# Other order of the loads, sums and transposes in the prologue of a hybrid conv and mLSTM block

## The chip, the cores and the metric

The kernel runs on one core of a Trainium2 chip. The metric is the device time of one execution in microseconds (us), lower is better; the time of a kernel is the median of its runs. In the rows, PE is TensorE's matrix multiplication, PEld its loading of weights, DVE VectorE, ACT ScalarE, POOL GpSimd, SP the engine that issues the DMAs. All times in rows count from the start of the profiled span.

## What is computed

One decoder block over x of 1024 tokens by 1024 channels, in float32. Only its beginning matters here:

```
mod = silu(c) @ w_ada + b_ada
sh1, sc1, g1, sh2, sc2, g2 = split(mod, 6)
h = rms_norm(x, norm_mix_g) * (1.0 + sc1) + sh1
proj = h @ w_in + b_in
```

`proj` feeds a gated convolution of 31 taps, an mLSTM over chunks and two gates; their merged output goes through `w_out`, and a SwiGLU feed-forward and a last RMSNorm follow. All that comes after the first columns of `proj` is the same text in both kernels.

## The kernel before

The channels lie on the 128 partitions, in 8 tiles of 128, and the 1024 tokens run along a row. Every large product is made three times: the left and the right operand are split into a high part of type float32r and the rest, named `hh` and `hl` for h, `whi` and `wlo` for weights (`wf` for the first two weight tiles), and high by high, high by low and low by high are added up.

The prologue makes `hh` and `hl` of h, and with them the first two column tiles of `proj`, so that the steady part, which begins with the products of L165, finds everything ready. It has these steps.

- **x**: four DMAs of 1 MB bring x, 256 tokens each, into the pairs `xt` (`xt_104` and `xt_106` hold the first 512 tokens, the other two the second). ScalarE squares each of the 8 token tiles with a sum along the row (L242, an ACTIVATE and an ACTIVATION_READ_ACCUMULATOR each). For each half of four tiles VectorE prepares the means (`rstd`, L244), GpSimd takes the power -0.5 (L111), and the four tiles are scaled in place (L251 on VectorE; the last of the eight on ScalarE, L249).
- **Transposes**: TensorE turns each half into channel tiles, four 128 by 128 transposes for each of the 8 channel tiles k (L255), into three PSUM buffers: one `pn` for k = 0, 3 and 6, two `pc` for the others. They are copied from there into the half rows of `xT` (L258), on ScalarE or VectorE as the letters of `EVAC` say, one string for each half.
- **Modulation**: `w_ada` for shift and scale is loaded in four groups g of 256 channels for each of the two (`wad`, 2 MB a group in four DMAs: rows 0 to 511 and 512 to 1023, for shift and for scale). VectorE sums a group's 8 row tiles, each times silu(c), into `macc` (the first at L282, the other seven at L284, each on top of the one before). TensorE sums the partitions with a column of ones (L290, the column products, 8 rows in the trace for 4 products), and ScalarE makes columns of shift and scale of that (L299, L300).
- **h**: for the two channel tiles of each group ScalarE makes `hh` (L304) and the full h in place (L307), VectorE subtracts the two into `hl` (L343). For the last group VectorE makes the full h (L347). The first two weight tiles are split into `wf`, high part on ScalarE (L155), low part on VectorE (L156).
- **First products**: for each group, 16 matmuls of `hh` (L315), then the next group's column products, then 8 matmuls of `hl`.

A scheduler orders each engine's instructions by readiness and priority; in the prologue the lists `on_v`, `on_s` and `on_t` are tied one behind the other (`in_turn`) for VectorE, ScalarE and TensorE. On the chip each engine takes its instructions in the order of the program. SP issues the loads in this order: the first two pairs of x, c, the last two pairs, `b_ada` and `mix_g`, the four DMAs of group 0 of `w_ada`, two weight tiles (`wraw`), then the groups 1 to 3.

Of the kernel before, what the change touches and what calls it, by code (L numbers as in the profile page):

```python
# [8 lines left out]
F32 = mybir.dt.float32  # L9
# [3 lines left out]
OP = mybir.AluOpType  # L13
# [3 lines left out]
D = 1024  # L17
# [18 lines left out]
EVAC = ("aaaaaaaa", "avaavaav")  # L36
# [19 lines left out]
def hybrid_block(ctx: ExitStack, tc: tile.TileContext, x, c, w_ada, b_ada, norm_mix_g, w_in, b_in,  # L56
# [140 lines left out]
    for i in range(4):  # L197
        t = pro.tile([128, 2, D], F32, name=f"xt{i}", tag=f"xt{i}")
        nc.sync.dma_start(t, x2[i * 256:(i + 1) * 256, :].rearrange("(a p) d -> p a d", p=128))
        xt += [t[:, 0, :], t[:, 1, :]]  # L200
    wad = []

    def load_ada(g):
        t = pro.tile([128, KT, 2, 256], F32, name="wad", tag="wad", bufs=4)
        for kh in range(2):
            for i in range(2):
                c0 = i * 1024 + g * 256
                nc.sync.dma_start(t[:, kh * 4:kh * 4 + 4, i, :],
                                  wada[kh * 512:(kh + 1) * 512, c0:c0 + 256].rearrange("(k p) e -> p k e", p=128))
        wad.append(t)  # L210
# [10 lines left out]

    def split_rest():
        for i in range(2):
            load_split(None, 0, KT, 0, *w_first[i], raw=raws[i])
# [11 lines left out]
    late_evac = {"v": [], "s": []}  # L236
    rstd = pro.tile([128, 3, 8], F32, name="rstd")
    xT = [big.tile([128, S], F32, name=f"xT{k}", tag="xb") if k < XB else pro.tile([128, S], F32, name=f"xT{k}") for k in range(KT)]
    for q in range(2):
        for t in range(4 * q, 4 * q + 4):  # L240
# [5 lines left out]
        for t in range(4 * q, 4 * q + 4):  # L246
            r = rstd[:, 1, t:t + 1]
            if SCALE[t] == "a":
                nc.scalar.activation(xt[t], xt[t], AF.Copy, scale=r)  # L249
            else:  # L250
                (nc.gpsimd if SCALE[t] == "p" else nc.vector).tensor_scalar(xt[t], xt[t], r, None, op0=OP.mult)  # L251
        for k in range(KT):
            p = ps_n() if k % 3 == 0 else ps_c()
            for t in range(4):
                nc.tensor.transpose(p[:, t * 128:(t + 1) * 128], xt[q * 4 + t][:, k * 128:(k + 1) * 128], ident)  # L255
            h = xT[k][:, q * 512:(q + 1) * 512]
            e = "s" if EVAC[q][k] == "a" else "v"
            ins = nc.scalar.activation(h, p, AF.Copy) if e == "s" else nc.vector.tensor_copy(h, p)  # L258
            if q and k > 1:
                late_evac[e].append(ins)  # L260
# [15 lines left out]

    def mod_sums(g):
        acc = pro.tile([128, 2, 256], F32, name="macc", tag="macc", bufs=MACC)
        parts = [[], []]
        for k in range(KT):  # L280
            if k < 1:
                ins = nc.vector.tensor_scalar(acc, wad[g][:, k], sc_c[:, k:k + 1], None, op0=OP.mult)  # L282
            else:
                ins = nc.vector.scalar_tensor_tensor(acc, wad[g][:, k], sc_c[:, k:k + 1], acc, op0=OP.mult, op1=OP.add)  # L284
            parts[k // 4].append(ins)
        return acc, parts
# [32 lines left out]
    on_v, on_s, on_t = [], [], []  # L319
    w_next = [None]  # L320
    hl = []
    acc, parts = mod_sums(0)
    on_v.append(parts[1])
    on_v.append(late_evac["v"])
    on_s.append(late_evac["s"])
    split_rest()
# [1191 lines left out]
```

## Time and profile before

| | |
|---|---|
| median of 3 runs | 1707.31 us (1704.89 to 1707.32) |
| the profiled execution | 1706.31 us, its span 1704.6 us |
| TensorE busy in the span | 1664.8 us (98%) |
| VectorE busy | 1310.5 us (77%) |
| ScalarE busy | 647.5 us (38%) |
| GpSimd busy | 59.5 us (3%) |
| start of the steady products (L165) | 61.55 us |

Shares over the whole span say little of the prologue, which is its first 61.55 us: there each engine has to be read by itself, in order of time, with what ended its idle time.

### The profile page before, as it was taken

How to read it: one execution, taken by the hardware profiler on the slowest of the kernel's cores; microseconds unless marked ns; L12 is line 12 of the kernel's file. 1: busy time of each engine (PE TensorE's matmuls, PEld its weight loads, DVE VectorE, ACT ScalarE, POOL GpSimd, SP SyncE). 2: the span in 40 equal slices, each digit the busy share in tenths (PEclk: the TensorE clock that was granted, in tenths of full speed). 3: DMA queues.
4: the chain of work that ended last, by engine and by line, in shares of the span. 5: the costliest groups of instructions: out<-in, count | busy, mean ns of one | idle time of the engine just before them, and what ended most of it. 6: DMA issues, size and time to landing. Idle time of an engine off the chain costs nothing. (4 is left out here: it accounts for less than half of the span.)

```text
span 1704.6 us, 20805 instructions
## 1 busy us (share of the span) xinstructions
PE 1664.8 (98%) x8237; PEld 1394.9 (82%) x8237; DVE 1310.5 (77%) x1760; ACT 647.5 (38%) x835; POOL 59.5 (3%) x116
## 2 busy tenths in 40 slices
PE   5999999999999999999999999999999999999998
PEld 4798888888888889888888778888888888788886
DVE  6989998997699759637699567877767777667776
ACT  7425335322532253224521356422222222344344
POOL 0000001000000000000000000000000000000001
PEclk9999999999999999999999999999999999999999
DMA  9221121122112211224497543333332333495872
GB/s 325 64 63 49 38 62 38 50 62 75 38 39 73 62 38 50 75 82 155 129 374 283 189 160 130 112 105 100 99 104 93 101 98 110 144 355 188 283 248 110
DMA packets 221241, 211.12 MB, mean 124 GB/s; under 512 B 8455, under 2 KB 175127, under 8 KB 221143
## 3 DMA queue, kind: packets, MB, share of 16 engines
q1 hardware_dynamic: 202327, 164.70, 31.3%
q10 hardware_dynamic: 18576, 44.31, 6.9%
q8 instruction: 64, 1.05, 0.3%
q0 software_dynamic: 240, 0.79, 0.1%
q14 instruction: 34, 0.28, 0.0%
HBM read 168.60 MB, written 41.16 MB: 123 GB/s over the span
## 5 line engine op out<-in xcount | busy, mean ns | idle before, releaser
L395 DVE SCALAR_TENSOR_TENSOR cacc<-a,col,cacc 128x1024 f32<-128x1024 f32 x240 | 306.1, 1282 | 3.9 <-ACT cacc L393 1.4
L165 PE MATMUL mm<-hh,wlo 128*128 128x512 f32 x864 | 271.2, 391 | 1.6 <-DVE wlo L156 1.6
L165 PE MATMUL mm<-hl,whi 128*128 128x512 f32 x864 | 272.5, 392 | 0.0
L165 PE MATMUL mm<-hh,whi 128*128 128x512 f32 x864 | 271.6, 392 | 0.0
L165 PEld LDWEIGHTS mm<-hh,wlo 128*128 128x128 f32 x864 | 160.4, 188 | 33.7 <-DVE wlo L156 2.8
L165 PEld LDWEIGHTS mm<-hl,whi 128*128 128x128 f32 x864 | 161.0, 188 | 32.1 <-issue 0.5
L165 PEld LDWEIGHTS mm<-hh,whi 128*128 128x128 f32 x864 | 160.5, 188 | 31.6
L155 ACT ACTIVATE whi<-wraw 128x1024 fp32r<-128x1024 f32 x61 | 64.7, 1060 | 227.4 <-PE mm L165 176.1
L156 DVE TENSOR_TENSOR wlo<-wraw,whi 128x1024 fp32r<-128x1024 f32 x61 | 74.3, 1219 | 28.7 <-ACT whi L155 25.2
L1123 PE MATMUL mm<-Bh,gh 128*128 128x512 f32 (+1 forms) x192 | 71.5, 375 | 2.8 <-ACT gh L1060 1.4
L1124 PE MATMUL mm<-Bl,gh 128*128 128x512 f32 (+1 forms) x192 | 71.5, 373 | 0.7 <-DVE Bl L1042 0.7
L611 PE MATMUL mm<-wlo,hh 128*128 128x256 f32 x256 | 72.0, 282 | 0.0
L1125 PE MATMUL mm<-Bh,gl 128*128 128x512 f32 (+1 forms) x192 | 71.2, 371 | 0.0
L1215 ACT ACTIVATE wd<-reg 128x1024 fp32r<-128x1024 f32 (+1 forms) x36 | 35.2, 988 | 82.6 <-DVE reg L1339 54.2
L542 DVE SCALAR_TENSOR_TENSOR cacc<-qkraw,col,cacc 128x1024 f32<-128x1024 f32 x48 | 61.5, 1281 | 4.9 <-ACT cacc L540 4.5
L1366 PE MATMUL mm<-wd,xl 128*128 128x512 f32 (+1 forms) x154 | 59.6, 387 | 1.2 <-DVE xl L1347 1.2
L1365 PE MATMUL mm<-wd,xh 128*128 128x512 f32 (+1 forms) x154 | 59.6, 387 | 0.0
L1367 PE MATMUL mm<-wd,xh 128*128 128x512 f32 (+1 forms) x154 | 59.5, 386 | 0.0
L610 PE MATMUL mm<-whi,hh 128*128 128x256 f32 x192 | 54.5, 284 | 0.0
L612 PE MATMUL mm<-whi,hl 128*128 128x256 f32 x192 | 54.2, 283 | 0.0
L1347 DVE TENSOR_TENSOR xl<-xr,xh 128x1408 fp32r<-128x1408 f32 x27 | 43.7, 1619 | 8.7 <-ACT xh L1346 8.7
L1216 DVE TENSOR_TENSOR wd<-reg,wd 128x1024 fp32r<-128x1024 f32 (+1 forms) x36 | 40.2, 1132 | 11.2 <-ACT wd L1215 11.0
(501 smaller groups left out, 3863.8 us busy)
## 6 DMA issues: line engine op xcount, KB each, us to landing
wraw<-in_w_in_dram SPq DMA_DIRECT2D x64, 512.0 KB
xr<-act_d SPq DMA_DIRECT2D x27, 704.0 KB
awt<-in_w_ada_dram SPq DMA_DIRECT2D x32, 512.0 KB
graw<-in_w_ffn_up_dram SPq DMA_DIRECT2D x24, 512.0 KB
act_d<-cg ACTq DMA_DIRECT2D x48, 256.0 KB
uraw<-in_w_ffn_up_dram SPq DMA_DIRECT2D x22, 512.0 KB
reg<-in_w_ffn_down_dram SPq DMA_DIRECT2D x20, 512.0 KB
other<-in_w_ffn_down_dram SPq DMA_DIRECT2D x20, 512.0 KB
```

The source lines that it names most:

```text
L155: nc.scalar.activation(hi, raw, AF.Copy)
L156: (eng or nc.vector).tensor_sub(lo, raw, hi.bitcast(F32))
L165: nc.tensor.matmul(flat(acc)[:, a:b], lhs[:, k, :], rhs[k][:, a:b], start=(first and k == 0), stop=(last and k == kt - 1))
L395: nc.vector.scalar_tensor_tensor(acc, a[:, j:j + S], dw_col(j, ct), acc, op0=OP.mult, op1=OP.add)
L542: nc.vector.scalar_tensor_tensor(cv, raw[:, j:j + S], wcol(j), cv, op0=OP.mult, op1=OP.add)
L611: nc.tensor.matmul(o[:, 0:256], hh[k][:, ts_], los[k], start=False, stop=False)
L1123: nc.tensor.matmul(o, a, rh, start=(k == 0), stop=False)
L1124: nc.tensor.matmul(o, a, rl, start=False, stop=False)
L1125: nc.tensor.matmul(o, b, rh, start=False, stop=(k == 3))
L1365: nc.tensor.matmul(o, xh, wh, start=(k == 0), stop=False)
L1366: nc.tensor.matmul(o, xl, wh, start=False, stop=False)
L1367: nc.tensor.matmul(o, xh, wl, start=False, stop=(k == FP - 1))
```

## The change

Five things are moved. The first half of `w_ada`'s group 0 is loaded between the first and the second half of x, the second half of it behind x in quarters. Group 0 is summed in two parts: four row tiles directly behind the first half's scaling, the others between the scalings of the second half. The squares of the second half are tied behind the first half's last evacuation on ScalarE, and their roots are taken for two tiles at a time. The evacuations are dealt out in another way: of the first half four of eight go to VectorE (none before), of the second half one (three before). The high parts of `wf` are made by VectorE. And of the second half's transposes, k = 0 to 2 stand ahead of the column products of group 0, k = 3 to 5 behind them, and k = 6 and 7 behind the first 16 products.

```diff
-EVAC = ("aaaaaaaa", "avaavaav")
+EVAC = ("avavavav", "avaaaaaa")
...
+    def ada_rows(t, g, k0, n):
+        for i in range(2):
+            c0 = i * 1024 + g * 256
+            nc.sync.dma_start(t[:, k0:k0 + n, i, :],
+                              wada[k0 * 128:(k0 + n) * 128, c0:c0 + 256].rearrange("(k p) e -> p k e", p=128))
...
+    x_pair(0)
+    x_pair(1)
     param_columns(param_rows(6, [("b_ada", as_rows(b_ada, 48), 48), ("mix_g", as_rows(norm_mix_g, 8), 8)], rows[:, 1]))
-    load_ada(0)
+    ada0 = ada_tile()
+    ada_rows(ada0, 0, 0, 4)
+    x_pair(2)
+    x_pair(3)
+    ada_rows(ada0, 0, 4, 2)
+    ada_rows(ada0, 0, 6, 2)
...
+    def roots(a, b):
+        for t in range(a, b):
             junk = ps_mm()
-            nc.scalar.activation(flat(junk), xt[t], AF.Square, accum_out=rstd[:, 0, t:t + 1])
-        ms, rs, sc = (rstd[:, i, 4 * q:4 * q + 4] for i in range(3))
-        nc.vector.tensor_scalar(ms, ms, 1.0 / D, EPS, op0=OP.mult, op1=OP.add)
+            ins = nc.scalar.activation(flat(junk), xt[t], AF.Square, accum_out=rstd[:, 0, t:t + 1])
+            if t == 4:
+                queue_behind(ins, turned_s[-1])
+        ms, rs = (rstd[:, i, a:b] for i in range(2))
+        ins = nc.vector.tensor_scalar(ms, ms, 1.0 / D, EPS, op0=OP.mult, op1=OP.add)
+        if a == 4:
+            queue_behind(ins, turned_v[-1])
         rsqrt(rs, ms)
...
+    roots(0, 4)
+    for t in range(4):
+        scale(t)
+    for k in range(KT):
+        turn(0, k)
+    acc = mod_sums(0, range(4))
+    roots(4, 6)
+    scale(4)
+    scale(5)
+    mod_sums(0, range(4, 6), acc)
+    roots(6, 8)
+    scale(6)
+    scale(7)
+    mod_sums(0, range(6, 8), acc)
...
-    split_rest()
+    for k in range(3):
+        turn(1, k)
     p, ins = mod_products(0, acc)
+    on_t.append(ins)
+    for i in range(2):
+        on_v.append([nc.vector.tensor_copy(w_first[i][0], raws[i])])
+    for i in range(2):
+        on_v.append([nc.vector.tensor_sub(w_first[i][1], raws[i], w_first[i][0].bitcast(F32))])
...
             on_s.append([high(k)])
+            if g == 0:
+                for j in ((3,), (4, 5))[k]:
+                    turn(1, j)
...
         on_t.append(first_products(g, 0))
+        if g == 0:
+            turn(1, 6)
+            turn(1, 7)
```

`turn(q, k)` is one channel tile of one half: its four transposes and its evacuation. `scale`, `mod_sums` and the other functions do what the lines before did; VectorE's parts of them are put into `on_v` in the order of the text.

On VectorE, between the scaling of the first half of x and the sums of group 1 of the modulation, this stood before (from the roots of the second half on; `xT` is x transposed):

```order
L244 TENSOR_SCALAR rstd<-rstd 128x4
L282 TENSOR_SCALAR macc<-wad,sc_c 128x512
L251 TENSOR_SCALAR xt_108<-xt_108,rstd 128x1024 x2
L251 TENSOR_SCALAR xt_110<-xt_110,rstd 128x1024
L284 SCALAR_TENSOR_TENSOR macc<-wad,sc_c,macc 128x512 x4
L258 COPY xT_149<-pc 128x512
L284 SCALAR_TENSOR_TENSOR macc<-wad,sc_c,macc 128x512
L156 TENSOR_TENSOR wf_125<-wraw,wf_124 128x1024
L284 SCALAR_TENSOR_TENSOR macc<-wad,sc_c,macc 128x512
L156 TENSOR_TENSOR wf_129<-wraw,wf_128 128x1024
```

Two more sums' parts and two evacuations follow there until group 1. In the changed kernel the same stretch of VectorE ends with these rows, ahead of the sums of group 1:

```order
L277 COPY xT_157<-pc 128x512
L260 TENSOR_SCALAR rstd<-rstd 128x2
L270 TENSOR_SCALAR xt_118<-xt_118,rstd 128x1024 x2
L292 SCALAR_TENSOR_TENSOR macc<-wad,sc_c,macc 128x512
L260 TENSOR_SCALAR rstd<-rstd 128x2
L292 SCALAR_TENSOR_TENSOR macc<-wad,sc_c,macc 128x512
L270 TENSOR_SCALAR xt_120<-xt_120,rstd 128x1024
L292 SCALAR_TENSOR_TENSOR macc<-wad,sc_c,macc 128x512 x2
L277 COPY xT_151<-pc 128x512
L365 CAST wf_126<-wraw 128x1024
L365 CAST wf_130<-wraw 128x1024
L367 TENSOR_TENSOR wf_127<-wraw,wf_126 128x1024
```

The roots and the scaling of the second half now stand behind the last evacuation of the first half (the copy into `xT_157`, which is k = 7), the sums' second part is dealt out around them, and two casts of a weight tile are new ahead of the subtractions.

On ScalarE, behind the first half's squares, the second half's squares came first before, and then the evacuations:

```order
L242 ACTIVATE mm,rstd<-xt_108 128x1024 x2
L242 ACTIVATE mm,rstd<-xt_110 128x1024 x2
L258 ACTIVATE xT_148<-pn 128x512
L258 ACTIVATE xT_149<-pc 128x512
L258 ACTIVATE xT_150<-pc 128x512
L249 ACTIVATE xt_110<-xt_110,rstd 128x1024
```

In the changed kernel the same place on ScalarE reads:

```order
L277 ACTIVATE xT_150<-pn 128x512
L277 ACTIVATE xT_152<-pc 128x512
L277 ACTIVATE xT_154<-pc 128x512
L277 ACTIVATE xT_156<-pn 128x512
L256 ACTIVATE mm,rstd<-xt_118 128x1024 x2
L256 ACTIVATE mm,rstd<-xt_120 128x1024 x2
L268 ACTIVATE xt_120<-xt_120,rstd 128x1024
```

The squares moved behind the four evacuations that ScalarE keeps of the first half (k = 0, 2, 4, 6), the last of which needs TensorE's transposes of k = 6. From the first products of the last group on, the order of all five engines is the same in both kernels.

## Rows read from the trace of the kernel before

**Rows 1.** Busy time of each engine (and instructions) in the prologue and in all that follows; the last columns are the granted clock of TensorE as a share of 2.4 GHz, the share of the DMA engines' time and GB/s.

```profile
0.00:61.55 61.55, 43.37 (x199) 34.14 (x199) 47.02 (x74) 44.66 (x69) 2.96 (x10) 0.94 0.78 247
61.55:1704.60 1643.05, 1621.39 (x8040) 1360.75 (x8039) 1263.47 (x1686) 602.85 (x766) 56.56 (x106) 1.00 0.37 119
```

**Rows 2.** VectorE in order of time from the last evacuation ahead of group 1 on: start, time from the first one's start to the last one's end, what, number, and in brackets the idle time ahead and what ended it (no bracket: none worth a row). The sums of the groups 1 and 2 begin at 28.77 and 37.13.

```profile
27.57 1.28 DVE L258 COPY xT<-pc 128x512 f32<-128x512 f32 x2
28.77 0.47 DVE L282 TENSOR_SCALAR macc<-wad,sc_c 128x512 f32<-128x512 f32 x1
29.27 5.48 DVE L284 SCALAR_TENSOR_TENSOR macc<-wad,sc_c,macc 128x512 f32<-128x512 f32 x7
34.67 2.55 DVE L343 TENSOR_TENSOR hl<-xT,hh 128x1024 fp32r<-128x1024 f32 x2
37.13 0.48 DVE L282 TENSOR_SCALAR macc<-wad,sc_c 128x512 f32<-128x512 f32 x1
...
43.04 2.55 DVE L343 TENSOR_TENSOR hl<-xT,hh 128x1024 fp32r<-128x1024 f32 x2
```

**Rows 3.** Busy time of VectorE (and instructions) in the stretch from the sums of group 1 to the end of the last subtraction of the prologue; then clock, DMA share and GB/s as in Rows 1.

```profile
28.77:60.27 31.50, 30.44 (x39) 0.89 0.57 173
```

**Rows 4.** VectorE in order of time ahead of that, from the first half's roots on.

```profile
10.71 0.17 DVE L244 TENSOR_SCALAR rstd<-rstd 128x4 f32<-128x4 f32 x1 [1.31 <-ACT mm L242]
12.03 2.74 DVE L251 TENSOR_SCALAR xt<-xt,rstd 128x1024 f32<-128x1024 f32 x4 [1.15 <-POOL rstd L111]
15.31 0.22 DVE L135 COPY col<-pa 128x56 f32<-128x56 f32 x1 [0.55 <-PE pa L132]
...
16.39 0.17 DVE L244 TENSOR_SCALAR rstd<-rstd 128x4 f32<-128x4 f32 x1 [0.38 <-ACT mm L242]
16.77 0.49 DVE L282 TENSOR_SCALAR macc<-wad,sc_c 128x512 f32<-128x512 f32 x1 [0.21 <-DMA wad<-in_w_ada_dram]
17.69 2.08 DVE L251 TENSOR_SCALAR xt<-xt,rstd 128x1024 f32<-128x1024 f32 x3 [0.43 <-POOL rstd L111]
19.68 3.11 DVE L284 SCALAR_TENSOR_TENSOR macc<-wad,sc_c,macc 128x512 f32<-128x512 f32 x4
...
23.31 0.74 DVE L284 SCALAR_TENSOR_TENSOR macc<-wad,sc_c,macc 128x512 f32<-128x512 f32 x1
23.97 1.22 DVE L156 TENSOR_TENSOR wf<-wraw,wf 128x1024 fp32r<-128x1024 f32 x1
25.11 0.74 DVE L284 SCALAR_TENSOR_TENSOR macc<-wad,sc_c,macc 128x512 f32<-128x512 f32 x1
```

**Rows 5.** ScalarE in order of time: the second half's last two squares, the first evacuation, the scaling of the last tile of x, and `hh` of group 0, behind its columns.

```profile
14.18 1.01 ACT L242 ACTIVATE mm<-xt 128x1024 f32<-128x1024 f32 x1
...
15.22 1.01 ACT L242 ACTIVATE mm<-xt 128x1024 f32<-128x1024 f32 x1
16.17 0.19 ACT L242 ACTIVATION_READ_ACCUMULATOR mm<-xt 128x1 f32 x1
16.26 0.57 ACT L258 ACTIVATE xT<-pn 128x512 f32<-128x512 f32 x1
16.74 1.06 ACT L258 ACTIVATE xT<-pc 128x512 f32<-128x512 f32 x2
17.69 1.15 ACT L249 ACTIVATE xt<-xt,rstd 128x1024 f32<-128x1024 f32 x1
...
29.57 2.38 ACT L304 ACTIVATE hh<-xT,sh,G 128x1024 fp32r<-128x1024 f32 x2
```

**Rows 6.** TensorE in order of time: transposes of the first half, four of the second half, the column products and first products of group 0.

```profile
14.85 0.42 PE L132 MATMUL pa<-ident,rows 128*128 128x128 f32 x1
15.07 0.42 PE L255 MATMUL pn<-ident,xt 128*128 128x128 f32 x1
...
16.89 1.11 PE L255 MATMUL pn<-ident,xt 128*128 128x128 f32 x4 [0.97 <-ACT xT L258]
17.80 1.91 PE L255 MATMUL pc<-ident,xt 128*128 128x128 f32 x8
19.50 1.06 PE L255 MATMUL pn<-ident,xt 128*128 128x128 f32 x4
20.36 1.91 PE L255 MATMUL pc<-ident,xt 128*128 128x128 f32 x8
...
23.94 0.60 PE L255 MATMUL pn<-ident,xt 128*128 128x128 f32 x4
...
27.70 1.05 PE L290 MATMUL pa<-ones_col,macc 128*128 128x1 f32 x8 [0.71 <-DVE macc L284]
30.87 6.27 PE L315 MATMUL mm<-hh,wf 128*128 128x512 f32 x16 [2.12 <-ACT hh L304]
```

**Rows 7.** The power -0.5 on GpSimd by shape, over the whole kernel: shortest, median and longest in ns, first and last start.

```profile
L111 POOL TENSOR_TENSOR ss<-ss,minus_half x8: 536/544/1481, 997.8 to 1050.2; 128x1 f32<-128x1 f32 x8
...
L111 POOL TENSOR_TENSOR rstd<-rstd,minus_half x2: 1018/1024/1029, 11.0 to 16.6; 128x4 f32<-128x4 f32 x2
```

**Rows 8.** Busy time of each engine in two short stretches, columns as in Rows 1 (the third number from the end is the granted clock).

```profile
20.00:21.00 1.00, 1.00 (x7) 1.00 (x6) 0.96 (x2) 0.74 (x2) 0.00 (x0) 1.00 1.21 288
31.00:33.00 2.00, 2.00 (x5) 1.63 (x6) 1.93 (x3) 2.00 (x3) 0.00 (x0) 0.50 1.09 348
```

**Rows 9.** TensorE in order of time, the 16 products of group 1.

```profile
40.05 4.16 PE L315 MATMUL mm<-hh,wf 128*128 128x512 f32 x16 [0.17 <-ACT hh L304]
```

More of the change, by code (lines that the diff above doesn't have):

```diff
@@ L234, in dw_col @@
         return cols["dw0"][:, r:r + 1] if r < 128 else cols["dw1"][:, r - 128:r - 127]
-    late_evac = {"v": [], "s": []}
     rstd = pro.tile([128, 3, 8], F32, name="rstd")
     xT = [big.tile([128, S], F32, name=f"xT{k}", tag="xb") if k < XB else pro.tile([128, S], F32, name=f"xT{k}") for k in range(KT)]
-    for q in range(2):
-        for t in range(4 * q, 4 * q + 4):
+    on_v, on_s, on_t = [], [], []
+    turned_s, turned_v = [], []
+    def roots(a, b):
+        for t in range(a, b):
             junk = ps_mm()
-            nc.scalar.activation(flat(junk), xt[t], AF.Square, accum_out=rstd[:, 0, t:t + 1])
-        ms, rs, sc = (rstd[:, i, 4 * q:4 * q + 4] for i in range(3))
-        nc.vector.tensor_scalar(ms, ms, 1.0 / D, EPS, op0=OP.mult, op1=OP.add)
-        rsqrt(rs, ms)
[L246 to L249, printed above, removed]
-            else:
[L251 to L260, printed above, removed]
@@ new lines, in roots, with scale @@
+            ins = nc.scalar.activation(flat(junk), xt[t], AF.Square, accum_out=rstd[:, 0, t:t + 1])
[5 more added lines that the diff above has]
+            queue_behind(ins, turned_v[-1])
+        rsqrt(rs, ms)
+    def scale(t):
+        r = rstd[:, 1, t:t + 1]
+        if SCALE[t] == "a":
+            nc.scalar.activation(xt[t], xt[t], AF.Copy, scale=r)
+        else:
+            on_v.append([nc.vector.tensor_scalar(xt[t], xt[t], r, None, op0=OP.mult)])
@@ new lines, in turn @@
+    def turn(q, k):
+        p = ps_n() if k % 3 == 0 else ps_c()
+        ins = [nc.tensor.transpose(p[:, t * 128:(t + 1) * 128], xt[q * 4 + t][:, k * 128:(k + 1) * 128], ident) for t in range(4)]
+        h = xT[k][:, q * 512:(q + 1) * 512]
+        on_act = EVAC[q][k] == "a"
+        out = nc.scalar.activation(h, p, AF.Copy) if on_act else nc.vector.tensor_copy(h, p)
+        if not q:
+            (turned_s if on_act else turned_v).append(out)
+        else:
+            on_t.append(ins)
+            (on_s if on_act else on_v).append([out])
@@ new lines, in mod_sums @@
+    def mod_sums(g, ks=range(KT), acc=None):
+        if acc is None:
+            acc = pro.tile([128, 2, 256], F32, name="macc", tag="macc", bufs=MACC)
+        parts = [[], []]
+        for k in ks:
+            if k < 1:
+                ins = nc.vector.tensor_scalar(acc, wad[g][:, k], sc_c[:, k:k + 1], None, op0=OP.mult)
+            else:
+                ins = nc.vector.scalar_tensor_tensor(acc, wad[g][:, k], sc_c[:, k:k + 1], acc, op0=OP.mult, op1=OP.add)
+            parts[k // 4].append(ins)
+        on_v.extend(part for part in parts if part)
+        return acc
@@ L275, in in_turn @@
                     queue_behind(ins, earlier)
[L277 to L286, printed above, removed]
     def mod_products(g, acc):
```

29 lines of the change are left out of this document (10 added, 19 removed).

## The prediction

> **What bounds the kernel now.** I read the busy times of the prologue and of the rest first. From 61.55 us on TensorE works 1621.39 of 1643.05 us [rows 1] and both kernels have the same order there, so whatever the prologue gains or loses is passed on whole. Inside the prologue TensorE is not the bound (43.37 of 61.55 us). VectorE is: followed in time, it has no idle time with a cause from 27.57 on [rows 2], and is busy 30.44 of the 31.50 us from 28.77 on [rows 3]; the rest are sub-0.1 us gaps inside the chained sums. Its order behind the sums of group 1 is unchanged. So the question is one number: when do the sums of group 1 begin? Before: 28.77. They have no wait on their load, and the same bytes are loaded ahead of it in both kernels.
>
> **Prices.** From one start to the next on VectorE: scaling a tile 0.66 ((2.74-0.75)/3), a link of a sum 0.66 if something else stands between, else 0.79 ((3.11-0.75)/3), the subtraction for `wf` 1.14, all from [rows 4] (0.75 is a scaling's or a link's own length there); an evacuation 0.60 and the first product of a sum 0.50 [rows 2]. ScalarE: a square 1.04, from the last square's start to its sum's end 1.14, an evacuation 0.48 to 0.57, the scaling 1.15 [rows 5]. TensorE: four transposes 0.87 apart in the first half (16.89, 17.80, 19.50, 20.36) against 0.60 long at 23.94 [rows 6]. An engine sees another's result 0.04 to 0.06 later.
>
> Two prices have no row. **The cast** of a 128x1024 weight tile to float32r on VectorE: between 0.66 (scaling, the same size, one source in SBUF) and 1.14 (subtraction, same size, two sources). Below 0.66 I exclude nothing but see no reason for it; it streams as many elements. I take 0.66, since it has one source as the scaling does. [...] **The root of two tiles** (128x2) on GpSimd: between 0.54 (128x1) and 1.02 (128x4) [rows 7]; 0.70 on a straight line.
>
> **The change part by part**, along VectorE from the first scaling at 12.03, which keeps its time (the small copies of `b_ada`, 15.31 to 16.01, move ahead into idle time: 0.7 saved, and their rows now wait behind 2 MB less).
>
> *First half.* Four scalings, the first two links, then evacuations and links in turn: k0 14.68, k1 15.18, copy k=1 15.84, k2 16.44, copy k=3 17.10, k3 17.70. The load covers this: it was there at 16.77 behind 4 MB of x [rows 4], now behind 2. TensorE's transposes come 0.22 earlier without the parameter rows at 14.85, and ScalarE takes k=0 at 15.31 instead of 16.26, so the `pn` buffer frees 0.95 earlier and the rest of [rows 6] moves up by that: k=3 15.94, k=5 done 18.76, k=6 18.55 to 19.61, k=7 done 20.4. So VectorE **waits** 0.44 for k=5 and 1.05 for k=7, and is free at 21.05.
>
> *Second half's roots.* Before, the squares were done at 16.36. Now they queue behind the evacuation of k=6 on ScalarE, 19.65: first square 20.14, second 21.18, its sum 22.32. VectorE has nothing else in front of it: **1.30 idle**. Then GpSimd: 0.25 to its start, 0.70, 0.03: **0.90 idle**, scalings at 23.33 and 23.99, link k4 24.65, second roots 25.31, link k5, **0.2 idle**, third scaling 26.29, k6 26.95, k7 27.74, free 28.40. These links' rows land well before that.
>
> *Evacuation, casts, `wf`.* ScalarE scales the last tile from 26.29 to 27.44; TensorE finishes k=0 at 27.94 and k=1 at 28.80 at 0.87 each. VectorE's copy of k=1 starts 28.84 (**0.44 idle**), casts at 29.44 and 30.10, subtractions at 30.76 and 31.90, and the sums of group 1 at **33.04**.
>
> *Sum.* 33.04 - 28.77 = 4.27 us. As a check: the stretch from 12.03 was 16.74 with about 1.57 idle [rows 4], 15.2 of work; now 16.7 of work (casts 1.32 and two more evacuations 1.20 from ScalarE, one more root, less the small copies and some chained links) and 4.3 idle. Even with no idle time it would end at 28.73, no earlier than now. That is why a gain looks shut out.
>
> *Costed at nothing.* Two more DMA issues on SP: SP works ahead of the sums, which wait for no load. ScalarE loses two splits but takes evacuations k=3 to 7 between the first `hh`: column products end about 30.6, `hh` follows 0.82 behind them as in [rows 5, 6] at 31.4, and with five evacuations the full h of k=0 is there by 36.4, before VectorE wants it at 33.04+5.9=38.9. TensorE puts k=3 to 5 (2.6 us) ahead of the 16 products (6.27) and k=6, 7 (1.74) behind them; at the slow pace the column products of group 1 (1.05) then end at 42.2, and the full h of group 1 follows 0.82 and three steps of `hh`'s length, 1.19, later at 46.6, where VectorE wants it at 33.04+14.27=47.3 (28.77 to 43.04 in [rows 2]). The cover is 0.7 us thin; beyond it each us would be lost.
>
> So 1706.31+4.27=1710.6 on the profiled execution's own time (span 1704.6 and 1.7 around it); that execution lies 1.0 below the median of the runs, so the median forecast is 1707.31+4.3=1711.6.
>
> **Rivals.**
>
> *A: TensorE's quick pace all along.* Four transposes took 1.06 to 1.11 and later 0.60 [rows 6], though the granted clock reads 1.00 already in the slow stretch, from 20 to 21 [rows 8]; the rows don't say why. At the quick pace, 0.87x0.60/1.06 or 0.5 apart, the waits for k=5 and k=7 fall to 0.1 together, the second squares' sum ends 1.11 earlier and the copy of k=1 no longer waits: group 1 at 31.49, **+2.7**, 1710.0. For it: the same work may run either way. Against: before, the quick pace came only behind 20.4, and the first half is done by then.
>
> *B: the cast at the dear end,* 1.14: +5.2, 1712.5. So far only the shape speaks against it.
>
> *C: not slower: the clock level.* TensorE stood idle for 2.12 us before the first products, the granted clock was 0.50 while they ran (31 to 33) [rows 8] and the 16 took 6.27 against 4.16 for the next 16 [rows 6, 9]. The transposes behind the column products fill that hole; if the clock holds, TensorE gains 2.1 there. With A's 2.7 this gives 1707.31+2.7-2.1=1707.9. It decides only if TensorE, not VectorE, sets the stretch from 28.77 to 60; [rows 3] leave VectorE 1 us of idle time in all of it, so TensorE's gain would be spent waiting. [...]
>
> **How the numbers follow.** Measurement tells about 0.2% from no change, 3.4 us. Forecast (+3.4 to +5) 0.53, B 0.17, A 0.18, C 0.12. The forecast and B are slower: 0.70. A and two thirds of C are within 0.2%: 0.26. Faster gets 0.04, C with more of the hole given back than the rows allow. The range leaves out most of C below and a tenth of B above: from A less a us of run to run spread, 1708.8, to B plus as much, 1713.6.
>
> **What would show it.** In the profile after: VectorE begins the sums of group 1 near 33 (31.5 under A, 34 under B); idle time of VectorE named to ScalarE's squares (1.3), to GpSimd's root (0.9 and 0.2) and to TensorE's transposes (about 1.9 in three); casts 0.75 long; no idle time of VectorE behind the sums of group 1; L165's products beginning near 65.8 and the span after that still 1643. It is wrong if the squares begin well before 20, if TensorE's column products of group 0 start before 28, or if the steady part is longer or shorter by more than a us.

## The result and the profile after

The changed kernel takes 1712.25 us in the median of 8 runs (1710.56 to 1712.93), the kernel before 1707.32 (1704.89 to 1708.56, also 8): a ratio of 1.0028, interval 1.0019 to 1.0036, so it is slower by 4.9 us. The profiled execution is one of 1711.98 us with a span of 1710.3. Behind the prologue the line numbers are 45 higher: the evacuations stand at L277, the casts at L365, `wf`'s subtraction at L367, the sums at L290 and L292, the first products at L354.

First the two parts of the span, split at the first product of the steady part, with busy time per engine and, third from the end, the granted clock of TensorE as a share of the full one (the trace gives this share and no frequency); they answer to [rows 1].

```profile
0.00:65.62 65.62, 45.01 (x198) 35.52 (x199) 49.74 (x79) 42.17 (x65) 3.82 (x11) 0.87 0.73 232
65.62:1710.30 1644.68, 1622.86 (x8040) 1362.27 (x8039) 1263.50 (x1686) 602.90 (x766) 56.33 (x106) 1.00 0.37 119
```

The prologue is 4.07 us longer (65.62 against 61.55), the rest 1.63 (1644.68 against 1643.05). VectorE in order of time shows the first of the two; the rows answer to [rows 4] and [rows 2].

```profile
14.68 0.48 DVE L290 TENSOR_SCALAR macc<-wad,sc_c 128x512 f32<-128x512 f32 x1
...
18.59 0.69 DVE L277 COPY xT<-pc 128x512 f32<-128x512 f32 x1
19.46 0.69 DVE L277 COPY xT<-pc 128x512 f32<-128x512 f32 x1 [0.18 <-PE pc L274]
21.72 0.17 DVE L260 TENSOR_SCALAR rstd<-rstd 128x2 f32<-128x2 f32 x1 [1.57 <-ACT mm L256]
22.71 1.42 DVE L270 TENSOR_SCALAR xt<-xt,rstd 128x1024 f32<-128x1024 f32 x2 [0.82 <-POOL rstd L111]
...
24.82 0.75 DVE L292 SCALAR_TENSOR_TENSOR macc<-wad,sc_c,macc 128x512 f32<-128x512 f32 x1
26.16 0.75 DVE L270 TENSOR_SCALAR xt<-xt,rstd 128x1024 f32<-128x1024 f32 x1 [0.59 <-DMA wad<-in_w_ada_dram]
26.83 1.53 DVE L292 SCALAR_TENSOR_TENSOR macc<-wad,sc_c,macc 128x512 f32<-128x512 f32 x2
28.73 0.69 DVE L277 COPY xT<-pc 128x512 f32<-128x512 f32 x1 [0.37 <-PE pc L274]
29.34 1.28 DVE L365 CAST wf<-wraw 128x1024 fp32r<-128x1024 f32 x2
30.54 2.35 DVE L367 TENSOR_TENSOR wf<-wraw,wf 128x1024 fp32r<-128x1024 f32 x2
32.81 0.48 DVE L290 TENSOR_SCALAR macc<-wad,sc_c 128x512 f32<-128x512 f32 x1
33.33 5.48 DVE L292 SCALAR_TENSOR_TENSOR macc<-wad,sc_c,macc 128x512 f32<-128x512 f32 x7
38.72 2.55 DVE L385 TENSOR_TENSOR hl<-xT,hh 128x1024 fp32r<-128x1024 f32 x2
```

The reader is to see the row of brackets: from 19.46 to 28.73 VectorE stops five times, and from 32.81 to its last pieces of the prologue (`wlo`, begun at 61.98) not at all. The sums of group 1 begin 4.04 later than at 28.77 [rows 2], and nothing of that comes back. One bracket misleads: the wait of 0.59 at 26.16 is put down to a load, but the scaling behind it needs the root, and GpSimd ends that one just ahead of it (24.94 + 1.19 = 26.13); the second profile of this kernel names GpSimd for the same 0.59. Here is GpSimd in order of time, against [rows 7]:

```profile
21.97 0.70 POOL L111 TENSOR_TENSOR rstd<-rstd,minus_half 128x2 f32<-128x2 f32 x1 [9.98 <-DVE rstd L260]
24.94 1.19 POOL L111 TENSOR_TENSOR rstd<-rstd,minus_half 128x2 f32<-128x2 f32 x1 [2.27 <-DVE rstd L260]
```

The two are of the same size, and the second takes 0.49 longer. It begins while VectorE is in a link of the sums (24.82 to 25.57), the first while VectorE stands idle. So it is with all 20 roots of two columns in the profiles of this document: the 8 that began with VectorE idle took 0.69 to 0.71, the 12 that began during such a link 1.13 to 1.20. No edit tests whether the link is the cause.

The longest wait, 1.57, is for ScalarE's squares. In ScalarE's own order they stand behind the evacuation of k=6, while before they were done ahead of the first evacuation [rows 5]:

```profile
19.02 0.60 ACT L277 ACTIVATE xT<-pn 128x512 f32<-128x512 f32 x1 [0.44 <-PE pn L274]
19.51 1.02 ACT L256 ACTIVATE mm<-xt 128x1024 f32<-128x1024 f32 x1
...
21.50 0.19 ACT L256 ACTIVATION_READ_ACCUMULATOR mm<-xt 128x1 f32 x1
```

TensorE, against [rows 6]:

```profile
15.98 1.12 PE L274 MATMUL pn<-ident,xt 128*128 128x128 f32 x4 [0.26 <-ACT xT L277]
16.89 1.66 PE L274 MATMUL pc<-ident,xt 128*128 128x128 f32 x8
18.38 0.60 PE L274 MATMUL pn<-ident,xt 128*128 128x128 f32 x4
18.82 0.60 PE L274 MATMUL pc<-ident,xt 128*128 128x128 f32 x4
23.56 0.45 PE L274 MATMUL pn<-ident,xt 128*128 128x128 f32 x1 [4.14 <-ACT mm L256]
...
26.97 0.87 PE L274 MATMUL pn<-ident,xt 128*128 128x128 f32 x2 [2.31 <-DVE xt L270]
27.64 1.91 PE L274 MATMUL pc<-ident,xt 128*128 128x128 f32 x8
...
33.36 4.76 PE L354 MATMUL mm<-hh,wf 128*128 128x512 f32 x16
...
47.23 1.05 PE L329 MATMUL pa<-ones_col,macc 128*128 128x1 f32 x8 [1.06 <-DVE macc L292]
```

The transposes of the first half end early (0.60 for four from 18.38 on). TensorE then stands idle for 4.14 and for 2.31, and later waits for VectorE (1.06 at 47.23): it isn't what sets the end. In short windows of the same profile the granted clock is half (0.50) over the second half's transposes of k = 0 to 5, and it falls again at 48 and at 276 to 282:

```profile
22.00:34.00 12.00, 7.95 (x34) 7.09 (x35) 10.26 (x15) 7.03 (x14) 1.86 (x2) 0.50 1.10 344
...
48.00:54.00 6.00, 5.92 (x21) 4.50 (x21) 5.69 (x8) 5.42 (x8) 0.00 (x0) 0.72 0.55 149
...
276.00:278.00 2.00, 1.56 (x11) 1.56 (x12) 1.71 (x5) 1.97 (x3) 0.10 (x1) 0.89 0.83 230
278.00:280.00 2.00, 2.00 (x12) 2.00 (x11) 1.29 (x5) 2.00 (x6) 0.00 (x0) 0.50 0.01 2
280.00:282.00 2.00, 2.00 (x15) 2.00 (x15) 2.00 (x4) 2.00 (x5) 0.00 (x0) 0.75 0.00 0
```

One thing in the clock column misleads. The trace records the granted clock only from 18.2 on in this profile (from 15.7 to 31.8 in the 14 profiles of this document, and from 22.3 in the kernel before), and ahead of that a window prints 1.00 for want of a record; the 1.00 of [rows 8] at 20 to 21 is such a one. In the profiles whose record begins while transposes run, these pass within 0.1 us of that instant from the slow pace (0.21 from start to start) to the quick one (0.11). The slow pace is also that of the eight transposes at 27.64, where 0.50 is recorded. So the slow transposes early on most likely ran at half clock; no record says so.

Followed product by product, the changed kernel runs 4.1 us behind the kernel before up to 276, and 5.2 behind it from 282 on: the half clock there, at a place where the kernel before kept the full clock, costs about 1.1. Two rows of TensorE a little ahead of it, the first of the kernel before, say what it did: it waited for `kwl` of the mLSTM, 1.76 and 1.77.

```profile
272.38 0.50 PE L636 MATMUL pc<-vh,kwl 128*128 128x258 f32 x2 [1.76 <-DVE kwl L684]
...
276.44 0.50 PE L681 MATMUL pc<-vh,kwl 128*128 128x258 f32 x2 [1.77 <-DVE kwl L729]
```

Most of the remaining 0.5 is a longer wait for `whi` (1.84 at 978.80 against 1.24 at 973.09).

### The profile page after: what moved, and what is told of

Read it like the earlier page. It is cut to its first block, busy times and chain, and to the rows that moved or that the text cites. A ratio compares the mean times of both kernels' runs of the same rounds, so it can differ in the third digit from the quotient of the medians.

```text
span 1710.3 us, 20807 instructions
## 1 busy us (share of the span) xinstructions
PE 1667.9 (98%) x8237; PEld 1397.8 (82%) x8237; DVE 1313.2 (77%) x1765; ACT 645.1 (38%) x831; POOL 60.1 (4%) x117
## 3 DMA queue, kind: packets, MB, share of 16 engines
q8 instruction: 64, 1.05, 0.3%
## 5 line engine op out<-in xcount | busy, mean ns | idle before, releaser
L165 PE MATMUL mm<-hh,wlo 128*128 128x512 f32 x864 | 271.2, 391 | 1.5 <-DVE wlo L156 1.5
L165 PE MATMUL mm<-hl,whi 128*128 128x512 f32 x864 | 272.6, 392 | 0.0
L165 PE MATMUL mm<-hh,whi 128*128 128x512 f32 x864 | 271.5, 392 | 0.0
L165 PEld LDWEIGHTS mm<-hh,wlo 128*128 128x128 f32 x864 | 160.3, 188 | 33.6 <-DVE wlo L156 2.6
L165 PEld LDWEIGHTS mm<-hl,whi 128*128 128x128 f32 x864 | 161.0, 188 | 32.1 <-issue 0.5
L165 PEld LDWEIGHTS mm<-hh,whi 128*128 128x128 f32 x864 | 160.6, 188 | 31.6
L656 PEld LDWEIGHTS mm<-wlo,hh 128*128 128x128 f32 x256 | 49.1, 192 | 0.0
```

Source lines behind the costliest of these rows:

```text
L165: nc.tensor.matmul(flat(acc)[:, a:b], lhs[:, k, :], rhs[k][:, a:b], start=(first and k == 0), stop=(last and k == kt - 1))
L656: nc.tensor.matmul(o[:, 0:256], hh[k][:, ts_], los[k], start=False, stop=False)
```

## The experiments

The theory: VectorE's waits (for the squares first of all) and the casts make up the 4 us. Rivals: TensorE's new order, the new order of the loads, and, for the rest, an effect of the change on the steady part.

### Without the two ties

```diff
-            if t == 4:
-                queue_behind(ins, turned_s[-1])
...
-        if a == 4:
-            queue_behind(ins, turned_v[-1])
```

> The changed kernel without the two ties that hold the second half's squares and first roots behind the first half's last evacuations. Theory of the waits (VectorE's late start of the sums of group 1, 32.81 us, comes above all from the second half's squares queueing behind the evacuations): VectorE no longer stands idle for the squares and the sums of group 1 begin at 28.9 (28.3 to 29.5), the steady products at 61.7, and the kernel is back within 0.1% of the one before. Rival of the casts (the loss is VectorE's new work): sums of group 1 stay at 32 or later. Rival of TensorE's order (the loss is the transposes around the column products): no gain either, 32 or later.

1708.56 us, ratio 1.0006 (0.9997 to 1.0015) to the kernel before. VectorE in order of time:

```profile
17.11 0.16 DVE L258 TENSOR_SCALAR rstd<-rstd 128x2 f32<-128x2 f32 x1
...
18.58 1.42 DVE L266 TENSOR_SCALAR xt<-xt,rstd 128x1024 f32<-128x1024 f32 x2 [0.60 <-POOL rstd L111]
...
25.75 0.69 DVE L273 COPY xT<-pc 128x512 f32<-128x512 f32 x1 [0.28 <-PE pc L270]
26.35 1.28 DVE L361 CAST wf<-wraw 128x1024 fp32r<-128x1024 f32 x2
...
29.82 0.48 DVE L286 TENSOR_SCALAR macc<-wad,sc_c 128x512 f32<-128x512 f32 x1
```

The wait for the squares is gone, two waits of 0.60 and 0.28 are left, and the sums of group 1 begin at 29.82, 2.99 earlier than with the ties. That is 0.9 later than expected and outside the range of 28.3 to 29.5: without any idle time the work would end at 28.73, and the two waits add 0.88. The ties carry three quarters of the loss. The steady part, however, expected at 61.7, began only 1.58 earlier, at 64.04: VectorE's last piece of the prologue, `wlo`, came 2.98 earlier (59.00 against 61.98), and TensorE was now late, at a granted clock of 0.50 from 56 to 58.

### Without the ties, and the high parts of `wf` on ScalarE

```diff
-        on_v.append([nc.vector.tensor_copy(w_first[i][0], raws[i])])
+        nc.scalar.activation(w_first[i][0], raws[i], AF.Copy)
```

> The changed kernel without the two ties and with the high parts of the first two weight tiles on ScalarE again. Theory of the waits with the casts priced by the profile at 0.60 each: sums of group 1 at 27.7 (27.0 to 28.4), steady products at 60.5, 1.1 us ahead of the kernel before, whole kernel 1706 (1705 to 1707.3). If the casts were the larger part, this one gains 3 us or more over the untied one; if they cost nothing, it equals the untied one.

```profile
28.75 0.48 DVE L286 TENSOR_SCALAR macc<-wad,sc_c 128x512 f32<-128x512 f32 x1
...
61.55 0.73 PE L165 MATMUL mm<-hh,whi 128*128 128x512 f32 x2
```

The sums of group 1 begin at 28.75 and the steady part at 61.55, both as before the change (expected were 27.7 and 60.5, a gain that didn't come): 2.99 from the ties and 1.07 from the casts make up the whole loss of the prologue. All that is left of the change here, the loads, TensorE's order and the other evacuations, comes to nothing when taken together. Each of the two figures is a difference of two single profiles, and such differences are good to some 0.4: the changed kernel's own second profile has the sums at 33.16, and the version with all transposes ahead, below, has them at 32.42. Yet the kernel took 1714.07 us, ratio 1.0033 (1.0021 to 1.0045): the rest was 1651.35 long. The scheduler had written the later stages in another order, with a wait of 2.90 for `gh` at 1045 (1.41 in the kernel before) and with half clock at 272 to 278, 306 to 312, 1044 to 1052 and 1078 to 1082. The time expected was 1706; a total alone would have said that the casts help.

### The kernel before with seven useless casts

Seven casts of `wf`'s weight tiles, not used, are put on VectorE ahead of its sums of group 1.

```diff
+        for i in range(7):
+            nc.vector.tensor_copy(w_first[i % 2][1], raws[i % 2])
```

> The kernel before with seven useless casts of a weight tile on VectorE ahead of the sums of group 1 (their result is overwritten). Theory that VectorE's stretch is passed on whole: 7 x 0.60 = 4.2 us, steady products at 65.8 (65.4 to 66.4, up to 0.5 more where a cast waits for its weights), the whole kernel 4.2 to 5.2 us longer, the upper end if the later dip of TensorE's clock near 277 us comes here too (that dip is then a matter of when the steady part begins, not of this change). Rival that the stretch has slack: steady products before 64.5.

1711.91 us, ratio 1.0028 (1.0019 to 1.0037). Pairs of casts took 1.28 to 1.29, so one 0.69 and 0.60 from start to start; seven are 4.2 us, and VectorE's `wlo` came 3.95 later (61.88):

```profile
61.88 1.21 DVE L353 TENSOR_TENSOR wlo<-wraw,whi 128x1024 fp32r<-128x1024 f32 x1
```

The first product of group 1's sums begins at 30.58, since the scheduler moved the two subtractions for `wf` behind it; the links that follow go on at 33.24, 3.97 later than in the kernel before. That a delay of VectorE at this place is passed on, all but 0.25 of it, is shown without any of the change's own edits. The steady part began 5.29 later, more than the range expected, again with TensorE at half clock, from 58 to 60. At the wait for `kwl` (to 277.66) the clock held, so a late start alone doesn't bring the dip there.

### All transposes ahead of the column products

```diff
-    for k in range(3):
+    for k in range(KT):
         turn(1, k)
...
-            if g == 0:
-                for j in ((3,), (4, 5))[k]:
-                    turn(1, j)
...
-        if g == 0:
-            turn(1, 6)
-            turn(1, 7)
```

> The changed kernel with all eight of the second half's transposes ahead of the column products of group 0, as before the change. Theory of the waits: the sums of group 1 still begin at 32.8, and the full h of group 0 becomes late on ScalarE (about 40.0 against VectorE's wish at 38.7), so the steady products begin 1 to 2.5 us later than 65.6, at 66.6 to 68. Rival of TensorE's order: without transposes around the column products the loss goes, steady products near 61.6 to 63.

1712.33 us, ratio 1.0025 (1.0016 to 1.0034). The sums of group 1 begin at 32.42, and VectorE has no wait at its first `hl` (38.33): where TensorE's transposes stand makes no difference that counts to VectorE, in either direction. The sums are 0.39 earlier since in this profile the quick pace began at 16.3 and VectorE had no wait for k=5 and k=7. The steady part began at 66.64, 1.02 later and as late as expected, but not by the road expected: VectorE's `wlo` came 0.39 earlier, and TensorE ran at half clock from 56 to 62.

### The loads in the order of before

```diff
-    x_pair(0)
-    x_pair(1)
+    for i in range(4):
+        x_pair(i)
...
-    ada0 = ada_tile()
-    ada_rows(ada0, 0, 0, 4)
-    x_pair(2)
-    x_pair(3)
-    ada_rows(ada0, 0, 4, 2)
-    ada_rows(ada0, 0, 6, 2)
+    load_ada(0)
```

> The changed kernel with the loads issued in the order of before: all of x, then the parameter rows, then the modulation rows of group 0; the rest is as changed. If the order of VectorE's work is what costs, and not the loads, the sums of group 1 still begin between 32.0 and 33.2 (32.81 in the changed kernel) and the time is within 1 us of the changed kernel's, near 1712. Before, the rows of group 0 were there at 16.77 and the first link of them would now want them at about 15, so up to 1 us of waiting may show there, with the second half's squares then no later, since they wait for ScalarE. Rival: the later half of x (2 MB behind the first rows) is what holds the squares of the second half back; then with the loads back the squares begin before 19 and the sums of group 1 at 29 to 31.

1711.15 us, ratio 1.0024 (1.0015 to 1.0033); the sums of group 1 at 32.39, as the theory has it. The first product of the sums, begun at 17.60 behind two evacuations (14.68 with the early loads), didn't wait for its rows, and the links now fill the time in which VectorE had waited for the squares; these are done when it asks for them, at 21.31. So loading the rows earlier buys nothing in this order. The squares began at 18.93, right behind the evacuation of k=6 as in the changed kernel, and the sums not at 29 to 31, so the rival falls. The steady part began at 66.69, again with half clock from 56 to 62.

### Only the high parts back on ScalarE

The edit of the second experiment alone, with the ties kept.

> The changed kernel with the two high parts of wf made by ScalarE again, as before, and nothing else undone. If each cast costs VectorE 0.6 to 0.7 and nothing else follows from it, the sums of group 1 begin at 31.5 to 31.8 (32.81 less 1.07 to 1.3), the first products of the stage behind the prologue about 1.1 us earlier than 65.62, and the time is near 1711. Rival: ScalarE's two splits (1.2 us each) fall between its evacuations and delay the last scaling or the column products; then the sums of group 1 begin no earlier than 32.4.

The sums of group 1 at 31.15, 1.66 earlier (31.5 to 31.8 expected): 1.21 for the two casts, and 0.45 since the first half's transposes came quicker this time (VectorE at the roots by 21.27, not 21.72). The steady part began at 63.98 (1.64 earlier), but the time, expected near 1711, was 1712.30, ratio 1.0027 (1.0016 to 1.0037): its rest is 1646.6 long, with half clock at 274 to 280 and at 1042 to 1052.

### Free order: no ties, no copies and no casts on VectorE in the first half

To the edits of the second experiment this adds

```diff
-EVAC = ("avavavav", "avaaaaaa")
+EVAC = ("aaaaaaaa", "avaaaaaa")
```

> The changed kernel without the two ties (the second half's squares and sums need not stand behind the first half's evacuations), with the first half evacuated by ScalarE alone as before, and with the high parts of wf on ScalarE. VectorE loses four evacuations (2.4) and two casts (1.07) and the waits for TensorE and for the squares. Theory: the sums of group 1 begin at 26 to 28, ahead of 28.77 in the kernel before; the stage behind the prologue begins at 59 to 61, and, its order being that of before in all but two rows, the time is 0 to 2 us below the kernel before's, 1705.5 to 1707.5. Rival one: ScalarE with eight evacuations becomes the bound and the second squares end late, then the sums of group 1 begin at 29 or later. Rival two: VectorE's gain is spent waiting for TensorE's products (pa), whose clock falls to half after idle time, and the stage begins at 61.5 or later, time 1707 to 1709.

1708.42 us, ratio 1.0009 (1.0000 to 1.0018). The theory's 26 to 28 was wrong: the sums of group 1 began at 29.50. VectorE waited 2.44 for the transpose of k=1, and TensorE's row says for whom:

```profile
24.62 1.12 PE L270 MATMUL pn<-ident,xt 128*128 128x128 f32 x4 [3.03 <-ACT xT L273]
```

ScalarE had put the last scaling and the first high part ahead of the evacuation of k=6, whose buffer these transposes need. This is rival one by another road. Rival two shows too: the steady part began at 63.62, 4.95 behind `wlo`, with half clock from 52 to 58 behind an idle stretch of 1.05, and the time is within its 1707 to 1709.

### The same, with ScalarE put in order

```diff
-EVAC = ("aaaaaaaa", "avaaaaaa")
+EVAC = ("aaaaaaaa", "aaaaaaaa")
...
-            nc.scalar.activation(xt[t], xt[t], AF.Copy, scale=r)
+            scaled_s.append(nc.scalar.activation(xt[t], xt[t], AF.Copy, scale=r))
+            queue_behind(scaled_s[-1], turned_s[-1])
...
-        nc.scalar.activation(w_first[i][0], raws[i], AF.Copy)
+        ins = nc.scalar.activation(w_first[i][0], raws[i], AF.Copy)
+        queue_behind(ins, scaled_s[-1])
```

> A version built from what the runs so far showed: the changed kernel without the two ties, all transposed tiles evacuated by ScalarE, the high parts of wf on ScalarE too, and on ScalarE the last scaling held behind the first half's evacuations and the two high parts behind that scaling (in the version tried last a high part ran ahead of two evacuations, and TensorE waited 3.03 for them). Theory: VectorE has none of the waits for TensorE left, the sums of group 1 begin at 26.5 to 27.5 (28.77 in the kernel before, 29.50 in the version tried last), VectorE waits up to 1 us at the first hl for ScalarE's full h, and the first hl begins at 33.0 to 34.0 (34.67 before). Each us gained there is passed on if TensorE's clock holds: the stage behind the prologue begins at 60 to 61 and the time is 1706 to 1707.5. Rival: TensorE, done sooner with each group, stands idle before the next column products for more than the 0.3 to 0.4 of before, its clock falls late in the prologue as it did at 52 to 58, and the stage begins at 61.5 to 62.5: time 1707 to 1709, no version of this order beats the kernel before.

1707.35 us, ratio 0.9999 (0.9990 to 1.0008). VectorE did what was expected: sums of group 1 at 27.27, `wlo` at 56.62, 1.31 earlier than in the kernel before. Still the steady part began at 61.75, 0.20 later. TensorE in order of time, and two of its short windows:

```profile
50.45 1.05 PE L326 MATMUL pa<-ones_col,macc 128*128 128x1 f32 x8 [0.80 <-DVE macc L289]
...
61.75 0.73 PE L165 MATMUL mm<-hh,whi 128*128 128x512 f32 x2
```

```profile
50.00:52.00 2.00, 1.47 (x10) 1.35 (x11) 1.90 (x3) 0.46 (x3) 0.00 (x0) 1.00 0.45 107
52.00:54.00 2.00, 2.00 (x7) 1.51 (x6) 2.00 (x3) 2.00 (x5) 0.00 (x0) 0.50 0.00 0
```

Behind an idle stretch of 0.80 the clock falls to half (0.50 at 52 to 54), ten us ahead of the first steady product, and the products that follow are late. The rival was right: VectorE's gain is spent by TensorE. But such a stretch doesn't always do it. In the version without ties and casts TensorE stood idle for longer at the same place, and the clock held:

```profile
51.55 1.05 PE L325 MATMUL pa<-ones_col,macc 128*128 128x1 f32 x8 [1.07 <-DVE macc L288]
```

```profile
52.00:54.00 2.00, 1.91 (x11) 1.33 (x10) 1.90 (x3) 1.36 (x5) 0.00 (x0) 1.00 0.00 0
```

So it was with 1.05 at 53.95 in the version without casts. In all, the profiles have 14 idle stretches of 0.80 to 1.07 ahead of the column products of groups 2 and 3; the clock fell behind eight of them.

### The same, with the hole filled

Six useless transposes of the identity stand on TensorE ahead of the column products of group 3.

```diff
+        if g in (2,):
+            junk = ps_n()
+            on_t.append([nc.tensor.transpose(junk[:, j * 128:(j + 1) * 128], ident, ident) for j in (0, 1, 2, 3, 0, 1)])
         if g < 3:
             p, ins = mod_products(g + 1, acc)
```

> The version before (all evacuations and the high parts of wf on ScalarE, sums of group 1 at 27.27) with six useless 128x128 transposes of the identity on TensorE ahead of the column products of group 3, where it stood idle for 0.80 us at 50.45 and the granted clock fell to half at 52 to 56. They take 6 x 0.15 = 0.9 us at the quick pace and so fill the hole. Theory: it is that hole which lets the clock fall; filled, the clock stays at 1.00 there, the stage behind the prologue begins 3.6 behind VectorE's wlo as in the kernel before, at 60.2 to 60.5 instead of 61.75, and the time is 1705.5 to 1706.5, below the kernel before's by about 1 us. Rival: the clock falls there or a little later all the same (the holes of 0.3 to 0.4 that are left do it, or its fall has to do with something else), the stage begins at 61.7 or later and the time stays at 1707 to 1708.

1706.70 us against 1708.48 for the kernel before on the same chip, ratio 0.9987 (0.9978 to 0.9996): the one version whose interval lies below the kernel before. It overlaps with that of the version without the filling (0.9990 to 1.0008).

```profile
49.65 0.82 PE L411 MATMUL pn<-ident 128*128 128x128 f32 x6
50.53 1.05 PE L326 MATMUL pa<-ones_col,macc 128*128 128x1 f32 x8
...
60.55 0.73 PE L165 MATMUL mm<-hh,whi 128*128 128x512 f32 x2
```

```profile
52.00:54.00 2.00, 1.98 (x9) 1.38 (x8) 2.00 (x3) 2.00 (x5) 0.00 (x0) 1.00 0.00 0
```

Where the idle stretch was, the transposes now stand; the clock stays at 1.00, and the steady part begins 1.20 earlier with VectorE's `wlo` where it was (56.71). This is what the theory of the hole asks for (60.2 to 60.5 expected for the steady part). It isn't yet shown that the filling is what held the clock: there is one profile with the hole and one without, and the clock held behind longer holes in two other versions.

### Both kernels again

No edit: one more profile of the changed kernel, two more of the kernel before.

> The changed kernel once more, for a second profile. What is made in the prologue should repeat within 0.1 us: the sums of group 1 at 32.8, the stage behind it at 65.6. If the longer rest (1644.7 against 1643.05) comes from stretches at half clock whose place hangs on the instant, the stretch at 0.50 near 278 us need not stand there again, and the rest lies anywhere between 1643 and 1646. If it belongs to the order of the work, the same stretch shows the same dip and the same 1.04 us.

> The kernel before once more, for a second profile. If stretches at half clock behind the prologue hang on the instant and not on the order of the work, this one may show one of them where the first showed none (behind the wait for kwl near 272 or behind that for gh near 1040), with 1.0 to 1.7 us more from there on. If they belong to the changed order alone, its rest from the first product of the stage behind the prologue to the end is 1643.0 again, within 0.3.

> The kernel before a third time: as for the second profile. Theory: among the three the rest varies by up to 1.7 us with the place of the half clock; the prologue repeats within 0.2 us up to the sums of group 1 (28.77) and the stage behind it begins at 61.5. Rival: all three agree within 0.3 us in both parts.

The changed kernel: sums of group 1 at 33.16 (a wait of 0.34 for k=5 comes on top), steady part at 65.96, and half clock at 278 to 282 again. That is 0.35 later than the 32.8 that was to repeat within 0.1: the quick pace of the transposes began 0.6 later than in the first profile. The kernel before: 28.69 and 28.62, steady part at 61.51 and 61.40. Its second profile keeps the full clock near 272, as the first did. In its third it falls there, and the products, until then 0.17 earlier than in the first profile, come out 1.03 later behind it:

```profile
270.00:272.00 2.00, 0.45 (x4) 0.24 (x3) 2.00 (x4) 0.21 (x1) 0.10 (x1) 0.95 0.27 42
272.00:274.00 2.00, 1.79 (x8) 1.79 (x9) 1.55 (x5) 2.00 (x3) 0.00 (x0) 0.50 0.77 220
```

So that us isn't made by the change: the same program shows it or not, behind the same idle stretch of 1.76. The expected 0.2 us of repetition hold in the kernel before's prologue; its rest varies by some 1.4.

Over all 14 profiles the wait for `kwl` is the same (1.76 or 1.77), and the clock fell behind it in seven. They are not those with the latest start: the three that reached the steady part last (66.64, 66.69 and 66.84) kept the full clock there, and the version with ScalarE in order (61.75) did not. In the second profile of the changed kernel a further 1.5 of the rest is a longer wait for `gh` (2.61 at 1046.92 against 1.12 in the first; 1.01, 1.37 and 1.41 in the kernel before).

### All of them in one table

Times in us of each profiled run; the rest is the span less the start of L165. From 276 on TensorE's order is that of the kernel before only in the changed kernel, transposes ahead, loads of before and free order; only there is the rest that of the same work.

| version | sums of group 1 | `wlo` | half clock late in the prologue | L165 | rest | median |
|---|---|---|---|---|---|---|
| before, three profiles | 28.77, 28.69, 28.62 | 57.93, 57.86, 57.78 | none | 61.55, 61.51, 61.40 | 1643.1, 1642.4, 1643.8 | 1707.32 |
| changed, two profiles | 32.81, 33.16 | 61.98, 62.33 | 48 to 54 | 65.62, 65.96 | 1644.7, 1646.6 | 1712.25 |
| no ties | 29.82 | 59.00 | 54 to 60 | 64.04 | 1644.2 | 1708.56 |
| no ties, no casts | 28.75 | 57.92 | none | 61.55 | 1651.4 | 1714.07 |
| before and 7 casts | 30.58 (links 33.24) | 61.88 | 56 to 62 | 66.84 | 1643.4 | 1711.91 |
| transposes ahead | 32.42 | 61.59 | 56 to 62 | 66.64 | 1644.0 | 1712.33 |
| loads of before | 32.39 | 61.61 | 56 to 62 | 66.69 | 1642.6 | 1711.15 |
| no casts | 31.15 | 60.13 | none | 63.98 | 1646.6 | 1712.30 |
| free order | 29.50 | 58.67 | 52 to 58 | 63.62 | 1644.7 | 1708.42 |
| ScalarE in order | 27.27 | 56.62 | 52 to 56 | 61.75 | 1644.8 | 1707.35 |
| hole filled | 27.34 | 56.71 | none | 60.55 | 1644.7 | 1706.70 |

From `wlo` to L165 it is 3.62 to 3.85 where the clock held or had come back by 54, and 4.95 to 5.13 where it fell later: half clock late in the prologue costs 1.1 to 1.5, at 48 to 54 nothing.

## Why the prediction was right, and where it was off

**The bound.** VectorE sets the stretch: its delay at the sums of group 1 (4.04) and the one at the first steady product (4.07) agree, and seven casts put in by themselves were passed on too. L165 at 65.62 stands 0.2 from the forecast.

**The waits.** Their places were right; two sizes were not, and the misses cancel. The waits for k=5 and k=7 were priced at 0.44 and 1.05, at a slow pace of 0.87 per four transposes; the quick pace came at 18 and not behind 20.4, the squares began at 19.51 and not at 20.14, the copies waited 0.19 (begun at 18.59, and at 18.40 in the version without casts, where nothing held it) and 0.18, and VectorE reached the second half's roots 0.63 earlier than forecast (21.72 against 22.35). Rival A was thus half true. Its condition isn't a matter of the order: in the second and the third profile of the kernel before the first half's transposes ran at the quick pace from 16.8 on, the same text that ran them slowly in [rows 6]. Where the changed order met it (the version with all transposes ahead, roots at 21.34), the sums of group 1 began at 32.42 and not at A's 31.49, since the second half's transposes ran at half clock and the copy of k=1 still waited 0.36, and the second root took its 1.18. The squares cost 1.57 against 1.30, since VectorE was ready for them sooner. The second root was taken at 0.70, as the first indeed was, but took 1.19, beginning while VectorE was in a link, and its wait was 0.59 and not 0.2. The copy of k=1 waited 0.37 (0.44 forecast).

**The casts.** 0.60 from start to start, below the 0.66 taken, against 1.14 for `wf`'s subtraction of the same size in the same profile; rival B falls.

**The sum.** 33.04 forecast, 32.81 measured: -0.63 up to the roots, +0.49 by the second root, -0.12 by the casts, together -0.26 against the -0.23 measured. That the sum came so close is in part luck: two misses of half a us cancel, and the pace of the transposes, which decides the first, changes from profile to profile. Split by experiments, 2.99 belong to the ties and 1.07 to the casts, each to within some 0.4.

**The cover.** TensorE and ScalarE held. The cover said to be 0.7 us thin was wider, since the first products took 4.76 and not 6.27; in the changed kernel TensorE waits for VectorE at 47.23. The transposes didn't keep the clock up, as rival C hoped: it was at half from 22 to 34 already, having fallen within the 4.14 us of idle time. But the clock counted where VectorE was relieved: with VectorE 1.31 earlier, the steady part still began 0.20 later, behind a stretch at half clock (0.50 at 52 to 54). In the one profile of the last version, with six useless transposes in the hole, the clock stayed at 1.00 there and the steady part began 1.20 earlier.

**The step that failed** is "the span after that still 1643": it was 1644.68 and 1646.64, though both kernels have the same order there. About 1.1 of it is the half clock at 276 to 282, which the kernel before can have too (one profile in three); the second profile's further 2 us are for the most part the longer wait for `gh`. The medians differ by 4.93 where the prologue's loss is 4.07; the 0.9 between them is in the direction of these stretches. A later start doesn't make them likelier, by the versions that started later still and kept the full clock. Whether the change does in another way, or two profiles happened to show them, stays open. By its own criterion (longer by more than a us) the prediction was wrong in this term, and it came within 0.65 us of the time because the term is small.

## What to carry to other kernels

Where one engine is the bound, go along its order in the trace and ask of each instruction what it waits for now: a tie that puts the next input behind another engine's leftover copies cost more here (2.99 us) than the two added casts (1.07). When the bound engine is relieved, look at once at the next one, clock included: a fall of TensorE's clock ten us ahead of a hand-over ate a gain of 1.31 here, and with a few useless transposes in the hole ahead of it the gain was there in the one profile taken. Compare several profiles before laying such a fall to an edit. And judge an edit of one stage by that stage's own end, since a scheduler may write the later stages anew; with the half clock that came along, that was worth up to 8 us here.

## What was not expected of the hardware

TensorE's clock fell to half behind idle stretches of 0.8 to 1.8 us inside otherwise busy work, and not always: behind 8 of 14 stretches of 0.80 to 1.07 late in the prologue, and behind the same wait of 1.76 for `kwl` in 7 of 14 profiles, in one of three of the same program. What decides that, no row shows. A GpSimd root of two columns took 0.69 to 0.71 in 8 of 20 cases and 1.13 to 1.20 in the 12 in which VectorE was in a link of the sums as it began. And TensorE passed from the slow to the quick pace of transposes (1.12 to 0.60 for four) at another instant in each profile (16.3 to 22.3 where transposes ran just then), there where the record of the granted clock begins; the 1.00 that the windows print ahead of that is no measurement.
